# Layer B's q over all tokens as seven half-size block products, kept in DRAM, with z of the first token half ahead of it

## The chip, the core and the metric

The kernel runs on one core of a Trainium2 chip. The metric is device time in microseconds. Five engines matter here: TensorE (PE, its weight loads shown apart as PEld), VectorE (DVE), ScalarE (ACT), GpSimd (POOL) and SyncE (SP), which issues most DMAs. Each engine runs its own instructions in program order and waits on semaphores for the others.

## What is computed

1024 tokens of width 1024 in float32 pass one gated MLP layer (layer A), which also gives the shared k and v, and one sliding-window attention layer (layer B). The change touches layer B alone. Cut down, it is:

```python
h = h + rms_norm(gmlp_mixer(rms_norm(h, a_pre_g), ...), a_post_g)     # layer A
kv_in = rms_norm(h, kv_norm_g)
k, v = kv_in @ w_k, kv_in @ w_v                    # 4 heads of 64
q, z = jnp.split(rms_norm(h, b_pre_g) @ b_w_in, 2, axis=-1)
q = q * (HEAD_DIM ** -0.5)                         # 16 heads of 64
logits = q_block @ k_two_blocks.T + alibi          # blocks of 128, window 128
p = exp(logits - max(rowmax, sink)); denom = p.sum() + exp(sink - max)
o = (p @ v_two_blocks) / denom
h = h + rms_norm((o * jax.nn.silu(z)) @ w_out, b_post_g)
```

## The kernel before

**Arithmetic.** A float32 matrix product is made of three matmuls on operands split in two parts: hi, a copy rounded to the matmul's format (ACT, line 105 or 109), and lo, the rest (DVE, line 106 or 110). `mm3` issues hi by hi, hi by lo and lo by hi into one PSUM bank (lines 169 to 171). Layer A's three products are already seven half-size block products each for eight, with sums of blocks made on DVE and POOL by `add` (line 206). Layer B's are plain.

**Tokens.** The 1024 tokens are two halves of 512, h = 0 and 1. The normalised, transposed tokens of a half are `n`, a hi and lo tile of eight 128-row pieces by 512 tokens: `n0` comes from layer A's last stage, `n1` is made here. For n1 a token tile of 128 is scaled (`hb`, DVE, line 763), transposed by PE into PSUM (`nt`, line 769), and split into n_hi (ACT) and n_lo (DVE).

**Weights.** The class `Weights` holds a fixed list of 512 KB weight blocks in the order of use: q, kv, z for the first half, kv, q, z for the second, and at last the output weights. `wnext` hands out one block, splits the next into whi and wlo (lines 109 and 110, two of 128x512 each) and loads two further. Raw blocks live in a ring of three buffers, filled by SP's queue.

**Stages of layer B's front.** They are generators, so that a main stage can step a side stage between its groups of matmuls:

- `q_phase(0)`: 192 matmuls (`qz`, line 952 on). The side stage is `chain_a(1)`, the residual and norm of the second half's tokens (lines 746 to 758). Each of q's 128-row pieces leaves PSUM with a scale as hi (ACT, line 971) and lo (DVE, line 972) parts of 64 rows: q is kept as two tiles, each with hi in one half of its 128 rows and lo in the other.
- `kv_phase(0)`: k and v of the first half, with `norm_h1(1)` at its side.
- `z_phase(0)`: 192 matmuls; ACT takes z out of PSUM and applies SiLU (lines 981 and 984).
- `attn(0)`: eight units (two head groups by four blocks of 128 tokens). A unit is two score groups, each of eight matmuls (`s`, line 1050), DVE's masking and row maximum (lines 1055 and 1061) and ACT's exponentials (line 1065); a normalisation (lines 1070 and 1071); transposes (`pt`, line 1078) with POOL's selection (lines 1082 and 1083); values (`o`, lines 1097 and 1099); and the product with z and its split (lines 1103, 105 and 106). Stage i of the loop runs scores of unit i, transposes of unit i−1 and values of unit i−2. Between these, four calls of `more()` a stage step `fill`, which here is kv, q and half of z of the second half, 64 steps in all, spread evenly over 40 calls.
- `attn(1)` in the same way, with the rest of z and the output product of the first half as fill, and then the second half's output product to the end.

What sets the order: each engine's order is that of the generators' steps above, as the compiler's scheduler has arranged them; nothing at run time changes it. The names that recur below are `hb`, `n_hi`, `n_lo`, `q_slots` (a ring of result buffers), `qz`, `whi`, `wlo`, `raw_w`, `pr` (probabilities), `mx` and `dn` (row maximum and denominator), `kh`, `kl` and `vt` (k's parts and v).

Of the kernel before, what the change touches and what calls it, by code (L numbers as in the profile page):

```python
# [7 lines left out]
F32 = mybir.dt.float32  # L8
# [42 lines left out]
def tile_yoco(  # L51
# [60 lines left out]
    class Weights:  # L112


        def __init__(self):
            self.order = []
            q, z = ([(wqz[i, m:m + 4, :, kq * 256:kq * 256 + 256].rearrange("m p c -> p m c"), f"q{kq}")
                     for m in range(0, 8, 4) for kq in range(4)] for i in range(2))
# [3 lines left out]
            self.raw, self.done, self.at = [], [], 0  # L122

        def load(self, i):
            while len(self.raw) <= min(i, len(self.order) - 1):
# [4 lines left out]
        def split(self, i):  # L130
            while len(self.done) <= min(i, len(self.order) - 1):
# [627 lines left out]

    def norm_h1(h, n, yo, order=range(4)):  # L760
# [172 lines left out]
    bp = ctx.enter_context(tc.tile_pool(name="bp", bufs=1))  # L933
    bias = bp.tile([P, 4, P], F32, name="bias")
    nc.sync.dma_start(out=bias.rearrange("p a b -> p (a b)"), in_=consts[:, C_BIAS:C_BIAS + 512])
    mrg = bp.tile([P, P], F32, name="mrg")
    nc.sync.dma_start(out=mrg, in_=consts[:, C_MERGE:C_MERGE + P])
    neg = bp.tile([P, 1], F32, name="neg")
    nc.vector.memset(neg, -1e30)

    kh = [bp.tile([P, 2, S], F32R, name=f"kh{i}") for i in range(2)]

    kl = [bp.tile([P, 2, S], F32R, name="kl0")]
    qsc = bp.tile([P, 2], F32, name="qsc")
    nc.sync.dma_start(out=qsc, in_=consts[:, C_QS:C_QS + 2])
    snk = bp.tile([P, 4, 4], F32, name="snk")
    nc.sync.dma_start(out=snk.rearrange("p a b -> p (a b)"), in_=sinks.partition_broadcast(P))
    nc.vector.tensor_scalar(snk, snk, -1.0, None, ALU.mult)
    half = [slice(0, 64), slice(64, P)]
    vt = big.tile([P, NB, 256], F32, tag="P1_1", name="vt")  # L950

    def qz_four(h, which, m, n, evac):

        tag = "s" if (h, which, m) in ((0, 0, 4), (0, 1, 0)) else "mm"
        ps = [bank(tag, f"qz{h}_{which}_{m + i}") for i in range(4)]
# [10 lines left out]
    def q_phase(h, n, q):  # L966
        def evac(m, ps):
            for par in range(2):
                rw, ot = half[par], half[1 - par]
                g = qsc[rw, m // 4:m // 4 + 1]  # L970
                nc.scalar.activation(q[par][rw, m], ps[rw], AF.Copy, scale=g)
                nc.vector.scalar_tensor_tensor(q[par][ot, m], ps[rw], g, q[par][rw, m].bitcast(F32),  # L972
                                               ALU.mult, ALU.subtract)

        for m in range(0, 8, 4):
            yield from qz_four(h, 0, m, n, evac)

    def z_phase(h, n, z, m0, m1):
        def evac(m, ps):
            zt = z[m // 4]  # L980
            nc.scalar.activation(zt[:, m % 4], ps, AF.Copy)
            if m % 2 == 1:
                zs = zt[:, m % 4 - 1:m % 4 + 1]
                nc.scalar.activation(zs, zs, AF.Silu)

        for m in range(m0, m1, 4):
            yield from qz_four(h, 1, m, n, evac)

    def kv_phase(h, n):
        pk = [bank("mm", f"pk{h}_{i}") for i in range(2)]  # L990
        pv = [bank("mm", f"pv{h}_{i}") for i in range(2)]
# [114 lines left out]
    def attn(h, q, z, fill, total, late=0):  # L1106
        taken = [0, 0]
        n = 34 if late else 40
# [8 lines left out]
        for i in range(len(units) + 2):  # L1117
# [5 lines left out]
            more()  # L1123
            if 0 <= i - 1 < len(units):
# [79 lines left out]
    side = chain_a(1, yo, ss)  # L1204
    q0 = pair("P0", "q0")
    main = q_phase(0, n0, q0)
    step(main, main)
    for _ in main:
        step(side)
    drain(side)  # L1210
# [83 lines left out]
```

## Time and profile before

| what | us |
|---|---|
| median of 3 runs | 1050.68 |
| lowest and highest run | 1050.01, 1051.42 |
| the profiled execution | 1051.56 |
| its span in the trace | 1049.8 |

The mean granted TensorE clock of the profiled execution is 0.998. A trace row for one instruction gives its start, its length, engine, line, operation and tiles, and in brackets the idle time before it with what ended that. Matmuls overlap in PE's pipeline, so the distance from one start to the next, not the length, is what one costs. A row of groups ends with busy time and mean length in ns, then idle time before and its releaser. The stages in the trace: q of the first half from 654.1, kv from 697.6, z from 723.4, attention of the first half from 769 to 894.7, of the second half to 1005, then the rest of the output product to 1043 and the last stores.

### The profile page before, as it was taken

The numbers are of one execution on the slowest core, as the hardware profiler recorded it, in microseconds if no ns is written. First come the engines' busy times: TensorE is split into PE (matmuls) and PEld (weight loads), VectorE is DVE, ScalarE is ACT, GpSimd is POOL, SyncE is SP. The second block draws the span as 40 slices with busy tenths as digits, with TensorE's granted clock in tenths as the row PEclk, the third lists the DMA queues.
The fourth block names the chain that finished last, engine by engine and source line by source line (L and its number), as shares of the span: only waits on it lengthen the run. The fifth ranks groups of instructions, "written<-read, shape, count | busy, mean of one in ns | idle before, by whom it ended". The sixth has DMA issues, their size and how long they took to land.

```text
span 1049.8 us, 13661 instructions
## 1 busy us (share of the span) xinstructions
PE 1039.2 (99%) x4994; PEld 854.8 (81%) x4994; DVE 731.9 (70%) x1244; ACT 577.2 (55%) x989; POOL 195.2 (19%) x153
## 2 busy tenths in 40 slices
PE   9999999999999999999999999999999999999997
PEld 7888788888888888888888888888888777877776
DVE  6997466867768668677697587665247776667763
ACT  6683444555465565555444464654466665786631
POOL 0300003253342542530200000100001111011120
PEclk9999999999999999999999999999999999999999
DMA  8877252334333333347897642532222121211363
GB/s 310 271 282 269 101 177 88 116 105 143 124 121 116 132 124 117 108 137 272 322 352 270 201 160 93 200 102 86 95 81 71 51 81 61 81 61 61 121 220 120
DMA packets 80899, 157.56 MB, mean 150 GB/s; under 512 B 5824, under 2 KB 32704, under 8 KB 80832
## 3 DMA queue, kind: packets, MB, share of 16 engines
q1 hardware_dynamic: 76176, 147.75, 41.2%
q10 hardware_dynamic: 4656, 8.94, 2.4%
q8 instruction: 39, 0.64, 0.3%
q14 instruction: 28, 0.23, 0.1%
HBM read 125.21 MB, written 31.46 MB: 149 GB/s over the span
## 4 chain that ended last, share of the span: by engine, by line
PE 93%; DVE 4%; ACT 1%; issue 0%; DMA 0%; POOL 0%; DVEq 0%; POOLq 0%; ACTq 0%
PE ob L169 6%; PE ub L169 6%; PE ub L171 6%; PE ob L171 6%; PE ob L170 6%; PE ub L170 6%; PE qz L169 5%; PE qz L171 5%; PE qz L170 5%; PE uc L169 3%; PE uc L171 3%; PE uc L170 3%; PE s L1050 3%; PE sp L614 3%; PE vb L170 2%; PE vb L171 2%
## 5 line engine op out<-in xcount | busy, mean ns | idle before, releaser
L110 DVE SCALAR_TENSOR_TENSOR wlo<-raw_w,gn,whi 128x512 fp32r<-128x512 f32 x80 | 58.7, 758 | 62.2 <-ACT whi L109 62.0
L169 PE MATMUL qz<-n_hi,whi 128*128 128x512 f32 x256 | 101.0, 394 | 0.4 <-DVE q_lo L972 0.4
L171 PE MATMUL qz<-n_hi,wlo 128*128 128x512 f32 x256 | 100.0, 391 | 1.2 <-DVE wlo L110 1.2
L170 PE MATMUL qz<-n_lo,whi 128*128 128x512 f32 x256 | 99.8, 390 | 0.0
L109 ACT ACTIVATE whi<-raw_w,gn 128x512 fp32r<-128x512 f32 x80 | 54.9, 716 | 54.2 <-PE qz L170 35.0
L1065 ACT ACTIVATE pr<-pr,mx 128x129 f32<-128x129 f32 x128 | 50.0, 393 | 40.1 <-DVE mx L1061 40.0
L169 PEld LDWEIGHTS qz<-n_hi,whi 128*128 128x128 f32 x256 | 48.0, 188 | 16.6 <-issue 6.5
L105 ACT ACTIVATE uzhilo_g<-f 128x1024 fp32r<-128x1024 f32 x31 | 32.9, 1060 | 48.6 <-PE uc L171 42.7
L171 PEld LDWEIGHTS qz<-n_hi,wlo 128*128 128x128 f32 x256 | 48.0, 188 | 12.3 <-DVE wlo L110 2.1
L170 PEld LDWEIGHTS qz<-n_lo,whi 128*128 128x128 f32 x256 | 48.1, 188 | 9.3
L106 DVE TENSOR_TENSOR uzhilo_g<-f,uzhilo_g 128x1024 fp32r<-128x1024 f32 x31 | 39.0, 1257 | 19.9 <-ACT uzhilo_g L105 19.9
L209 ACT ACTIVATE uz_slots<-ub 128x512 f32<-128x512 f32 x48 | 28.3, 590 | 42.4 <-PE ub L171 39.0
L169 PE MATMUL ub<-T,whi_g 128*128 128x512 f32 x128 | 50.7, 396 | 0.0
L169 PE MATMUL ub<-T,uzhilo_g 128*128 128x512 f32 x128 | 50.5, 395 | 0.0
L171 PE MATMUL ub<-T,wlo_g 128*128 128x512 f32 x128 | 49.9, 390 | 0.0
L171 PE MATMUL ub<-T,uzhilo_g 128*128 128x512 f32 x128 | 49.9, 390 | 0.0
L170 PE MATMUL ub<-T,uzhilo_g 128*128 128x512 f32 x128 | 49.8, 389 | 0.0
L170 PE MATMUL ub<-T,whi_g 128*128 128x512 f32 x128 | 49.8, 389 | 0.0
L169 PE MATMUL uc<-T,uzhilo_g 128*128 128x512 f32 x124 | 48.9, 395 | 0.0
L170 PE MATMUL uc<-T,uzhilo_g 128*128 128x512 f32 x124 | 48.3, 389 | 0.0
L171 PE MATMUL uc<-T,uzhilo_g 128*128 128x512 f32 x124 | 48.3, 389 | 0.0
L105 ACT ACTIVATE whi_g<-raw_uz 128x1024 fp32r<-128x1024 f32 (+1 forms) x31 | 26.5, 854 | 36.7 <-PE ub L170 15.6
(332 smaller groups left out, 3071.4 us busy)
## 6 DMA issues: line engine op xcount, KB each, us to landing
raw_uz<-in_wuz_in_dram SPq DMA_DIRECT2D x32, 512.0 KB, 3.4
raw_w<-in_wqz_dram SPq DMA_DIRECT2D x32, 512.0 KB, 3.5
td<-uz_slots SPq DMA_DIRECT2D x56, 256.0 KB, 2.2
orawP2a<-td SPq DMA_DIRECT2D x28, 512.0 KB, 4.0
raw<-in_wv_in_dram SPq DMA_DIRECT2D x17, 512.0 KB, 4.8
vg<-vd SPq DMA_DIRECT2D x8, 1024.0 KB, 5.4
orawP2b<-in_wo_a_dram SPq DMA_DIRECT2D x16, 512.0 KB, 7.7
vraw<-in_wv_in_dram SPq DMA_DIRECT2D x13, 512.0 KB, 4.4
```

The costliest lines, as they stand in the source:

```text
L105: nc.scalar.activation(hi, src, AF.Copy)
L106: nc.vector.tensor_tensor(lo, src, hi.bitcast(F32), ALU.subtract)
L109: nc.scalar.activation(hi, src, AF.Copy, scale=g)
L110: nc.vector.scalar_tensor_tensor(lo, src, g, hi.bitcast(F32), ALU.mult, ALU.subtract)
L169: nc.tensor.matmul(out, lhsT=a_hi, rhs=b_hi, start=start, stop=False, skip_group_check=True)
L170: nc.tensor.matmul(out, lhsT=a_hi, rhs=b_lo, start=False, stop=False, skip_group_check=True)
L171: nc.tensor.matmul(out, lhsT=a_lo, rhs=b_hi, start=False, stop=stop, skip_group_check=True)
L209: nc.scalar.activation(out, a, AF.Copy)
L614: nc.tensor.matmul(psv[:, n], lhsT=d["vg"][:, 4 * j + n, i * P:(i + 1) * P], rhs=d["wc"], start=True, stop=True)
L1050: nc.tensor.matmul(pss[par][:, g, w0:256], lhsT=q[par][:, m, bs_], rhs=w[par][:, p, ks], start=g + k == 0, stop=g + k == 2, skip_group_che ...
L1065: nc.scalar.activation(pr[:, i], pr[:, i], AF.Exp, bias=mx[:, i:i + 1], scale=-1.0, accum_out=dn[:, i:i + 1])
```

## The change

q is computed for both halves at once. The 1024 by 1024 weight matrix and the tokens are taken as two by two blocks of 512, and Strassen's scheme (in Winograd's form) makes seven block products for eight. In pieces:

- `z_phase(0)` runs first, where q's first half ran. Its result goes to DRAM (`zd`, four stores) and comes back after the k/v stage.
- At its side run `chain_a(1)` and, new, `norm_sums`: the work of `norm_h1(1)` and the sums of token blocks that the products need (T5, T6, T4, T7; T1 to T3 are parts of n0 and n1). For each of four token tiles these are three subtractions and three lo splits on DVE, four additions and subtractions on POOL, and three hi splits on ACT, beyond n1's own.
- `q_tiles`: four quads of two 128-row weight blocks; each has seven products of 12 matmuls. DVE scales the raw weights by the norm's gain, POOL makes the weight sums, ACT and DVE split them. Results are summed from PSUM in six buffers and stored to DRAM (`qd`, 16 stores). The weights of its first quad are fetched and prepared at steps 22 and 27 of z.
- Buffers for this (`qp`) are closed after q, and the pool `bp` (masks, sink constants, kh, kl) is opened after that; it stood ahead of q before.
- `reload_q` brings a half of q back, four pieces of 512 KB, and makes the scaled hi and lo parts, two ACT and two DVE operations of 64x1024 a piece. The first half's pieces 0 and 1 are started in `kv_phase(0)` and one more piece in each stage of `attn(0)`: 2 and 3 of the first half, then the four of the second.
- `attn(0)` has 32 steps of fill for 64, kv and half of z; four of them run ahead of its first unit.

```diff
             kv = [(wkv[kp], f"kv{kp}") for kp in range(4)]
-            self.order += q + kv + z + kv + q + z
+            self.order += z + kv + kv + z
...
+    def norm_sums(n, yo, first):
...
+        for t in (2, 3, 0, 1):
+            ts_ = slice(t * P, (t + 1) * P)
+            xt = st.tile([P, D], F32, tag="xt", name=f"hb1_{t}")
+            nc.vector.tensor_scalar(xt, yo[t], r1[1][:, t:t + 1], None, ALU.mult)
+            yield
...
+            for kq in range(2):
...
+                split(n[0][:, ks, ts_], n[1][:, ks, ts_], ps)
+                if kq == 0:
+                    add(t1, ps, n_0[0][0][:, :, ts_].bitcast(F32), ALU.subtract)
+                    add(t1, t1, n_0[1][0][:, :, ts_].bitcast(F32), ALU.subtract, nc.gpsimd)
+                else:
+                    add(t3[:, :, ts_], ps, n[0][:, 0:HT, ts_].bitcast(F32), ALU.subtract)
+                    add(t2, ps, t1, ALU.subtract)
+                    add(t4, n_0[0][1][:, :, ts_].bitcast(F32), t2, ALU.subtract, nc.gpsimd)
+                    add(t3[:, :, ts_], t3[:, :, ts_], n[1][:, 0:HT, ts_].bitcast(F32), ALU.subtract, nc.gpsimd)
+                    add(t4, t4, n_0[1][1][:, :, ts_].bitcast(F32), ALU.add, nc.gpsimd)
+                yield
+            for m, src in ((6, t2), (5, t1)):
+                split(T[m][0][:, :, ts_], T[m][1][:, :, ts_], src)
+            yield
+            split(T[4][0][:, :, ts_], T[4][1][:, :, ts_], t4)
+            yield
...
+        for i in range(2):
+            split(*(a[:, 2 * i:2 * i + 2] for a in T[7]), t3[:, 2 * i:2 * i + 2])
+        yield
...
-    def q_phase(h, n, q):
...
+    def q_tiles():
...
+        def scaled(r):
+            rv = r.rearrange("p (k c) -> p k c", k=KT)
+            add(rv, rv, gn[:, G_BPRE:G_BPRE + KT].unsqueeze(2).broadcast_to([P, KT, P]), ALU.mult)
...
+        def prep1(q):
+            if q < 4:
+                r0, r1 = raws[q]
+                ops[q] = {}
+                scaled(r0)
+                pieces_of(q, r0, "q1", 1, 2)
+                scaled(r1)
+
+        def prep2(q):
...
+                add(s1, a21, a22, ALU.add, nc.gpsimd)
+                add(s2, s1, a11, ALU.subtract, nc.gpsimd)
+                pieces_of(q, f, "q2", 6, 5)
+                add(s3, a11, a21, ALU.subtract, nc.gpsimd)
+                add(s4, a12, s2, ALU.subtract, nc.gpsimd)
...
+        for q in range(5):
...
+                product(q, 1, b, True)
...
+                product(q, 2, a, True)
+                add(c00, c00, a, ALU.add)
+                store(q, 0, 0, c00)
+                prep1(q + 1)
...
+            product(q, 6, b, False)
...
+            product(q, 5, cc, True)
+            prep2(q + 1)
+            fetch(q + 2)
+            product(q, 7, b, False)
...
+    def reload_q(h, q):
+
+        for i in range(4):
+            r = raw_tile(f"q{h}_{i}").rearrange("p (m t) -> p m t", m=2)
+            nc.sync.dma_start(out=r, in_=qd[h][i])
+            ms = slice(2 * i, 2 * i + 2)
             for par in range(2):
                 rw, ot = half[par], half[1 - par]
...
+                nc.scalar.activation(q[par][rw, ms], r[rw], AF.Copy, scale=g)
+                nc.vector.scalar_tensor_tensor(q[par][ot, ms], r[rw], g, q[par][rw, ms].bitcast(F32),
                                                ALU.mult, ALU.subtract)
...
-    def attn(h, q, z, fill, total, late=0):
+    def attn(h, q, z, fill, total, late=0, first=0, side=iter(())):
         taken = [0, 0]
+        for _ in range(first):
+            step(fill)
...
+            step(side)
             if 0 <= i - 1 < len(units):
                 units[i - 1].transposes()
...
-    main = q_phase(0, n0, q0)
+    side = chain(chain_a(1, yo, ss), norm_sums(n1, yo, n0))
...
+    main = z_phase(0, n0, z0, 0, 8, keep=True)
+    qs = q_tiles()
     step(main, main)
-    for _ in main:
+    for i, _ in enumerate(main):
         step(side)
+        if i in (22, 27):
+            step(qs)
     drain(side)
...
+    drain(qs)
+    qp_ctx.close()
...
-    fill = chain(kv_phase(1, n1), q_phase(1, n1, q1), z_phase(1, n1, z1, 0, 4))
-    attn(0, q0, z0, fill, 64)
+    fill = chain(kv_phase(1, n1), z_phase(1, n1, z1, 0, 4))
+    attn(0, q0, z0, fill, 32, first=4, side=chain(side, reload_q(1, q1)))
```

Two places show how the instructions stand on DVE. The first is where the second half's first token tile is scaled, beside q's matmuls before and beside z's now. In the rows `hb_2` is token tile 2 scaled, `r_1_90` the norm's factor, `wlo` the lo part of a weight block and `qz_0_0` q's first bank. Before:

```order
L178 TENSOR_SCALAR r_1_90<-s_1_4999 128x4
L763 TENSOR_SCALAR hb_2_5318<-yoa_3_4273,r_1_90 128x1024
L110 SCALAR_TENSOR_TENSOR wlo_5097<-raw_w_5024,gn,whi_5096 128x4x128 x2
L972 SCALAR_TENSOR_TENSOR q_hi<-qz_0_0_4959,qsc,q_hi 64x512
L763 TENSOR_SCALAR hb_3_5352<-yoa_3_4273,r_1_90 128x1024
L972 SCALAR_TENSOR_TENSOR q_hi<-qz_0_1_4960,qsc,q_hi 64x512
```

Now, further on in the same stage, with `qT_5055`, `qT_5056` and `qT_1_5058` the lo parts of T5, T6 and T4, and `t_3` the temporaries t1 and t2 of token tile 3:

```order
L208 TENSOR_TENSOR q_slots<-nt_3_1_5166,n_hi 128x4x128
L208 TENSOR_TENSOR t_3_5149<-nt_3_1_5166,t_3_5148 128x512
L106 TENSOR_TENSOR qT_5055<-t_3_5148,qT_5055 128x4x128
L110 SCALAR_TENSOR_TENSOR wlo_5196<-raw_w_5067,gn,whi_5195 128x4x128
L106 TENSOR_TENSOR qT_5056<-t_3_5149,qT_5056 128x4x128
L110 SCALAR_TENSOR_TENSOR wlo_5196<-raw_w_5067,gn,whi_5195 128x4x128
L106 TENSOR_TENSOR qT_1_5058<-q_slots,qT_0_5057 128x4x128
L779 TENSOR_SCALAR hb_0_5217<-yoa_2_4272,r_1_90 128x1024
L110 SCALAR_TENSOR_TENSOR wlo_5255<-raw_w_5128,gn,whi_5254 128x4x128 x2
L779 TENSOR_SCALAR hb_1_5284<-yoa_2_4272,r_1_90 128x1024
L106 TENSOR_TENSOR n_lo<-nt_0_0_5227,n_hi 128x4x128
L208 TENSOR_TENSOR t_0_5225<-nt_0_0_5227,n_hi 128x512
```

The evacuations of q (line 972) have left this stage; the sums, n's lo parts and T's lo parts have come in, and hb of tiles 0 and 1 stands behind T4's lo part of tile 3, whose source `q_slots` POOL writes.

The second place is DVE in the first half's attention. `pr`, `mx` and `s` are a unit's probabilities, maxima and scores, `z_0` the gate. Before:

```order
L1061 ISA pr_1_6365,mx_1_6366<-s_1_01_6370,bias,snk 128x128
L1061 ISA mx_1_6366 128x1
L1103 TENSOR_TENSOR z_0_5296<-o_0_6389,z_0_5296 128x4x128
L106 TENSOR_TENSOR q_lo<-z_0_5296,q_hi 128x4x128
L110 SCALAR_TENSOR_TENSOR wlo_6410<-raw_w_6281,gn,whi_6409 128x4x128 x2
L972 SCALAR_TENSOR_TENSOR q_hi<-qz_0_0_6207,qsc,q_hi 64x512
L1038 COPY pr_1_6495<-snk 128x8
L972 SCALAR_TENSOR_TENSOR q_lo<-qz_0_0_6207,qsc,q_lo 64x512
```

Now, in the third unit's stage:

```order
L1223 RECIPROCAL dn_0_6285<-dn_0_6285 128x8
L1214 ISA pr_0_6381,mx_0_6382<-s_0_00_6385,bias,snk 128x128
L1214 ISA mx_0_6382 128x1
L1224 TENSOR_TENSOR pr_0_6283<-pr_0_6283,dn_0_6285 128x8x128
L1214 ISA pr_0_6381,mx_0_6382<-s_0_00_6385,bias,snk 128x128
L1214 ISA mx_0_6382 128x1
L1125 SCALAR_TENSOR_TENSOR q_hi<-raw_q_3_6321,qsc,q_hi 64x1024
L1125 SCALAR_TENSOR_TENSOR q_lo<-raw_q_3_6321,qsc,q_lo 64x1024
L1214 ISA pr_0_6381,mx_0_6382<-s_0_01_6386,bias,snk 128x128
```

In place of the evacuations from PSUM, 16 of 64x512 for the second half, stand the splits of pieces that come back from DRAM (line 1125 of the changed kernel), 12 of 64x1024 in this attention, among the units' own operations.

More of the change, by code (lines that the diff above doesn't have):

```diff
@@ L973, in evac, with z_phase @@
                                                ALU.mult, ALU.subtract)
[L975 to L978 removed]
+            yield
+    def z_phase(h, n, z, m0, m1, keep=False):
         def evac(m, ps):
```

179 lines of the change are left out of this document (140 added, 39 removed).

## The prediction

> **What bounds the kernel now.** I read the page's busy times and its chain first, then busy time by stage, because a share of the whole says little about one stage.
>
> ```profile
> span 1049.8 us, 13661 instructions
> PE 1039.2 (99%) x4994; PEld 854.8 (81%) x4994; DVE 731.9 (70%) x1244; ACT 577.2 (55%) x989; POOL 195.2 (19%) x153
> PE 93%; DVE 4%; ACT 1%; issue 0%; DMA 0%; POOL 0%; DVEq 0%; POOLq 0%; ACTq 0%
> ```
>
> PE is busy in 99% of the span, and the chain that ended last runs over PE for 93% of it. So a matmul that goes shortens the time, as long as the other engines still keep ahead of PE. The windows show how near they are (window, its length, then busy time of PE, PEld, DVE, ACT and POOL, the granted clock, DMA).
>
> ```profile
> 26.20:52.50 26.30, 26.30 (x117) 21.43 (x116) 25.67 (x28) 15.79 (x21) 10.20 (x3) 1.00 0.81 271
> 654.00:697.60 43.60, 42.35 (x186) 34.44 (x185) 26.92 (x38) 22.36 (x38) 3.82 (x3) 1.00 0.48 162
> 723.40:769.00 45.60, 45.60 (x209) 37.97 (x208) 15.48 (x22) 22.30 (x35) 0.00 (x0) 1.00 0.32 104
> 769.00:894.70 125.70, 125.25 (x681) 99.70 (x680) 90.63 (x254) 81.38 (x215) 15.29 (x14) 1.00 0.21 68
> 1043.00:1046.00 3.00, 0.07 (x1) 0.00 (x0) 1.99 (x4) 0.69 (x2) 0.54 (x1) 1.00 0.00 1
> 1046.00:1049.80 3.80, 0.00 (x0) 0.00 (x0) 0.24 (x1) 0.00 (x0) 0.00 (x0) 0.58 0.38 140
> ```
>
> Layer B's first q stage (654 to 697.6) and z stage (723.4 to 769) leave DVE and ACT much room. In the first half's attention (769 to 894.7) DVE has work for 90.6 of 125.7 us: PE's matmuls of kv, q and z hide it. The change takes out the q part of that cover.
>
> **Part 1: matmuls removed, −10.9 us.** q over 1024 tokens is 2 × 192 matmuls before, and 4 × 7 × 12 = 336 after: 48 fewer of the same shape.
>
> ```profile
> 654.10 0.39 PE L169 MATMUL qz<-n_hi,whi 128*128 128x512 f32 x1
> 661.80 0.39 PE L170 MATMUL qz<-n_lo,whi 128*128 128x512 f32 x1
> ```
>
> PE's timeline has 34 starts from the first of these rows to the second: 7.70/34 = 0.2265 us each, and 48 × 0.2265 = 10.9 us. Other PE work is only moved: 32 transposes go from the kv stage into the z stage.
>
> **Part 2: the sums before q can start, +10 us (5 to 17).** q's products now need sums of both token halves. So the second half's normalisation (hb), its transposes, and the operands T4 to T7 must be done within the z stage, where there was slack. On DVE, between hb of tile 2 and the lo part of the first q weight (wlo_q_0, which the fifth matmul of q needs), stand 4 hb, 8 half weight splits (L110), 32 subtractions of 128x512 and 4 operations of 128x1024. Their prices are steps from one start to the next:
>
> ```profile
> 672.11 0.17 DVE L178 TENSOR_SCALAR r<-s 128x4 f32<-128x4 f32 x1 [1.28 <-ACT junk_h L183]
> 673.40 0.76 DVE L763 TENSOR_SCALAR hb<-yoa,r 128x1024 f32<-128x1024 f32 x1 [1.12 <-POOL r L179]
> 674.07 1.41 DVE L110 SCALAR_TENSOR_TENSOR wlo<-raw_w,gn,whi 128x512 fp32r<-128x512 f32 x2
> 704.71 1.29 DVE L106 TENSOR_TENSOR n_lo<-nt,n_hi 128x512 fp32r<-128x512 f32 x2
> 857.39 0.20 DVE L1070 RECIPROCAL dn<-dn 128x8 f32<-128x8 f32 x1 [0.90 <-ACT pr L1065]
> 857.63 1.23 DVE L1071 TENSOR_TENSOR pr<-pr,dn 128x1024 f32<-128x1024 f32 x1
> 858.78 1.41 DVE L110 SCALAR_TENSOR_TENSOR wlo<-raw_w,gn,whi 128x512 fp32r<-128x512 f32 x2
> ```
>
> hb takes 0.67 (673.40 to 674.07); a pair that lasts 1.41 with 0.75 for its second gives 0.66 for an L110; a pair of 1.29 gives some 0.61 for a 128x512 subtraction; 857.63 to 858.78 gives 1.15 for 128x1024. The sum is 2.7 + 5.3 + 19.5 + 4.6 = 32.0 us. It can't begin before hb of tile 2, at 673.4 in the trace, since the norm ahead of it is as it was: DVE is done at 705.4 at the earliest. PE comes to that matmul at 654.1 + 192 × 0.2265 + 4 × 0.87 (transposes) + 4 × 0.2265 = 702.0. So at least 3.4 us are lost even with DVE packed.
>
> It isn't packed: four POOL operations a tile stand between its DVE operations.
>
> ```profile
> L206 POOL TENSOR_TENSOR f<-raw_uz,raw_uz 128x512 f32<-128x512 f32 x15 | 19.2, 1281 | 127.2 <-DVE uzhilo_g L106 127.2
> L206 POOL TENSOR_TENSOR uz_slots<-uz_slots 128x512 f32<-128x512 f32 x17 | 27.7, 1631 | 0.5
> 301.25 2.16 POOL L206 TENSOR_TENSOR uz_slots<-uz_slots 128x512 f32<-128x512 f32 x1
> L105 ACT ACTIVATE q_hi<-z 128x512 fp32r<-128x512 f32 x8 | 5.0, 623 | 5.7 <-DVE z L1103 5.7
> L105 ACT ACTIVATE uzhilo_g<-f 128x1024 fp32r<-128x1024 f32 x31 | 32.9, 1060 | 48.6 <-PE uc L171 42.7
> ```
>
> Sixteen at 1.28 to 1.63 are 20.5 to 26.1 us. The first follows the first t1 on DVE at some 677.4. In DVE's order T4's lo of tile 3 stands ahead of hb of tile 0, so POOL idles behind its eighth operation until ACT's hi of T4 (0.62) and DVE's lo, hb, two L110, hb, n_lo and t1 (0.61 + 0.67 + 1.32 + 0.67 + 0.61 + 0.61) have passed: 5.1 us. POOL is then done at 703 to 709, and T4's lo, T7's two pieces and wlo_q_0 follow (0.61 + 3 × 1.15 = 4.1, and 0.6 of ACT): 708 to 713. I take 710.5, 8.5 us behind PE. A second, smaller wait is at q's matmul 31, on the first weight sums: from wlo_q_0 on, a scaled weight (1.15), three POOL operations (3.8 to 4.9), ACT's hi (1.06) and DVE's lo (1.15) take 7.2 to 8.3 us, against 26 matmuls, 5.9: 1.5 more. **The middle is +10**; the low end is 3.4 + 1.3, about 5 (POOL's part wholly hidden in the z stage), the high end has 16 × 0.4 us more, towards the 2.16 row, +17.
>
> The Trainium skill (SBUF — State Buffer, section "Who interferes with whom") says that a DVE instruction with two SBUF inputs contends with a GpSimd instruction that reads SBUF. The lo parts of T4 to T7 are such instructions. The rows 1281, 1631 and 2.16 for one operation are in keeping with that, though they don't show its cause; by the rule the sum would lie at the upper end of this part, without it near the lower.
>
> Once q runs, its DVE work (12 adds, 15 weight pieces, 7 scalings: 7.3 + 17.3 + 8.1 = 32.7 us) and POOL's 16 sums (20.5 to 26.1) lie beside 336 × 0.2265 = 76.1 us of matmuls: no further loss.
>
> **Part 3: attention without q's matmuls, +10 us (5 to 20).** Before, 64 steps of matmuls are spread over this attention; now 32, of which four run ahead of it, at the same rate per call. Six unit stages hold the last of them and five or six pieces of q reloaded from DRAM, each two ACT and two DVE operations of 64x1024.
>
> ```profile
> 716.97 0.40 PE L169 MATMUL pk<-n_hi,whi 128*128 128x512 f32 x1
> 719.79 0.40 PE L169 MATMUL pk<-n_hi,whi 128*128 128x512 f32 x1
> ...
> 702.41 0.87 PE nt L769 x8
> ...
> 846.74 0.94 PE s L1050 x8
> ...
> 859.91 1.01 PE o L1097 x4
> 860.93 0.86 PE o L1099 x4
> ...
> 659.71 2.48 DVE L753 SCALAR_TENSOR_TENSOR yoa<-yoa,rpa,xa 128x1024 f32<-128x1024 f32 x2 [1.19 <-POOL rpa L179]
> 838.06 0.76 DVE L1055 COPY_PREDICATED s<-mrg,s 128x256 f32<-128x256 uint32 x2
> 839.81 0.68 DVE L1103 TENSOR_TENSOR z<-o,z 128x512 f32<-128x512 f32 x1
> L1019 DVE TENSOR_TENSOR kl<-pk,kh 64x512 fp32r<-64x512 f32 x4 | 2.8, 688 | 0.5 <-ACT kh L1018 0.4
> ```
>
> PE in these six stages: 6 kv pairs of 2.82 (716.97 to 719.79), 16.9; 48 z matmuls, 10.9; 13 score groups of 0.94, 12.2; 5 transpose groups of 0.87, 4.4; values 6.6 (mostly 1.01 + 0.86); 51.0 us. DVE: 12.5 score groups of 1.75 (838.06 to 839.81), 21.9; 6 normalisations of 1.39 (857.39 to 858.78), 8.3; 8 gating operations and splits of 0.61, 4.9; 9 weight splits of 0.66, 5.9; 6 copies and subtractions for k and v of 0.61, 3.7; 12 reloads, for which the trace has only the 128x1024 form (2.48 for two, 1.2 from start to start), 14.4; 59.1 us. **DVE takes PE's place as the bound here.** Less two score groups (3.5 us) by which DVE may start ahead or end behind, 59.1 − 51.0 − 3.5, about 5 us, are lost with DVE packed. It wasn't packed before:
>
> ```profile
> DVE dn L1070 <- ACT pr L1065: 6.0, 7, 0.9
> ```
>
> Seven waits of the normalisation for the exponentials (0.9 us each at most) stood there at no cost to PE; six of them now count, 5 us: +10. The high end doubles the excess, where ACT and DVE wait for each other. The stage as a whole is near balance too: DVE 90.6, less 16 evacuations of q (0.74 each, 11.8) and 16 weight splits of q (11.3), plus 14.4, is 82; PE 125.7 less 43.5 (192 matmuls), less 5.6 (two kv pairs, now ahead), plus 7 for z matmuls that had run after, is 83.6.
>
> **Part 4: edges and DRAM, +0.5 us (0 to 3).** 16 stores of q, four of z, eight reloads of q and four of z stand on SP's queue, eight weight loads leave it.
>
> ```profile
> td<-uz_slots SPq DMA_DIRECT2D x56, 256.0 KB, 2.2
> raw_w<-in_wqz_dram SPq DMA_DIRECT2D x32, 512.0 KB, 3.5
> ```
>
> A store and its reload take 2.2 + 3.5 us, and the first half's kv (8 × 2.82 = 22.6 us) lies between the last store and the first scores. Behind a waiting reload stand the weight loads, two stages ahead of their use. The pool for masks and k/v begins where q's ends, so its constants load later, also in that cover; uncovered, one trip costs 5.7, of which I keep 3 as the high end.
>
> **Sum.** −10.9 + 10 + 10 + 0.5 = +9.6. The profiled execution took 1051.56 (its span and 1.8 around it), so 1061.2; the runs' median, 1050.68, is 0.88 lower: **1060.3 us**.
>
> **Rivals.** (a) *The cover holds* (faster): in 26.2 to 52.5 DVE was busy 25.67 of 26.30 us and PE lost nothing, so DVE can be packed. Then only 5 us (part 2's floor) and 2 us (waits at units' edges) are lost: −10.9 + 7 = −4, 1046.7. It decides if the two losses together stay under 10.9. Against it: that window has few instructions without waits between engines, here each tile goes DVE, PE, ACT, DVE, POOL, DVE. (b) *Only the z stage loses*: DVE's lead carries attention, −10.9 + 10 + 4 = +3, 1053.8. (c) *The clock falls too*: the last rows of the windows show a granted clock of 1.00 in the first 3 us without matmuls and 0.58 in the next 3.8. A wait of over 3 us before q would then slow the matmuls behind it: 0.42 × 3.8 = 1.6 us a gap, two or three gaps, and high ends of parts 2 and 3: 1066 to 1076. For it speaks the length of part 2's wait; against it that waits for single tiles may split it. The Trainium skill (TensorE: Matmul & The Clock Gate, section "What's actually happening") has the clock at half speed after an idle window of about 3.4 us; the two rows agree with it. (d) *The change doesn't do what it says*: no fewer matmuls issued, or a DRAM trip in the path each unit (8 × 2.2 = 18 us): above 1068.
>
> **How the numbers follow.** About 0.2% (2 us) is what a measurement of this kernel can tell from no change. Forecast (1055 to 1066) 0.47; (a) 0.20, of it 0.17 below 1048.5; between (a) and (b), 1048.5 to 1053, 0.08; (b) 0.12; (c) 0.10; (d) 0.03. Faster 0.20 with the edges of (a), same 0.08, slower 0.72. The sum's own ends are 1050 and 1080; the range 1046 to 1075 reaches down to (a) and leaves the far ends out.
>
> **What would show it.** Part 1: some 4946 matmuls, 0.2265 us apart. Part 2: a PE gap of 5 to 12 us where z ends, released by DVE (wlo_q_0 or T's lo), and POOL's sums back to back ahead of it. Part 3: between kv of the first half and the end of the z matmuls PE under 90% busy and DVE over 85%, with PE's scores and transposes released by DVE. If PE is full in that stretch, part 3 is wrong; if z's end has no gap, part 2 is wrong and the time falls below 1050. (c): granted clock under 0.95 behind the gap.

## The result, and the profile after

The changed kernel takes **1076.55 us** (median of 4 runs, 1074.9 to 1077.34) against 1050.78 (4 runs) of the kernel before on the same chip: a ratio of 1.0239, 95% interval 1.0227 to 1.0251, or 25.8 us slower. The forecast was slower by 9.6 us, 1060.3 us in a range of 1046 to 1075. The page of the changed kernel, first its span, the busy times and the granted clock, then the chain:

```profile
span 1075.6 us, 13692 instructions
PE 1041.8 (97%) x4946; PEld 850.4 (79%) x4946; DVE 768.6 (71%) x1258; ACT 587.1 (55%) x989; POOL 248.8 (23%) x185
...
PEclk9999999999999999999999999889999989999999
...
PE 83%; DVE 7%; ACT 4%; issue 3%; POOL 2%; DMA 1%; POOLq 0%; SPq 0%; DVEq 0%; ACTq 0%
```

The 48 matmuls are gone (4994 records before, 4946 now). PE fell from 99% to 97% of a longer span and from 93% to 83% of the chain: other engines now end PE's waits. Which waits, the table of PE's waits says (line, releaser: us in total, how many, the longest), from 640 to 935 us, which holds layer B's front and the first half's attention. First all that the kernel before has there, then the seven largest of the changed kernel:

```profile
PE qz L171 <- DVE wlo L110: 1.2, 2, 0.7
PE qz L169 <- DVE q_lo L972: 0.4, 1, 0.4
```

```profile
PE qb L171 <- ACT whi_q L105: 5.4, 1, 5.4
PE o L1250 <- POOL pc L1236: 4.7, 3, 2.3
PE z L173 <- DVE wlo L110: 4.6, 3, 3.3
PE pt L1231 <- DVE pr L1224: 3.7, 2, 2.0
PE s L1203 <- ACT pc L1232: 2.1, 2, 2.0
PE qc L171 <- ACT qhilo_q L105: 1.8, 1, 1.8
PE nt L787 <- DVE hb L779: 1.6, 1, 1.6
```

Four of them (`nt`, `z`, `qb`, `qc`) stand between the start of z and q's first quad, 13.4 us; three (`pt`, `s`, `o`) in the attention, 10.5 us. The stages by windows of the changed kernel (length, then busy time of PE, PEld, DVE, ACT and POOL, granted clock, DMA): z up to q's first matmul, q and the first half's k/v, the first half's attention, and the first 64.5 us of it apart.

```profile
654.00:717.50 63.50, 51.71 (x227) 40.91 (x225) 52.35 (x64) 33.29 (x58) 25.92 (x18) 0.92 0.35 127
717.50:827.50 110.00, 108.20 (x516) 90.89 (x517) 52.67 (x62) 43.30 (x59) 27.87 (x18) 0.97 0.42 142
827.50:927.80 100.30, 89.39 (x485) 66.11 (x483) 85.11 (x234) 77.71 (x199) 17.00 (x14) 0.95 0.24 79
827.50:892.00 64.50, 55.25 (x310) 41.85 (x309) 55.36 (x155) 47.62 (x127) 8.66 (x7) 0.92 0.25 83
```

DVE is busy for 52 of 63 us in the first of them, where before it had had 27 of 44. To compare kernels I count a stretch's **loss**: its length, less its matmuls at the prediction's prices (0.2265 us for 512 columns, some 0.118 for 256, 0.87 for eight transposes). Some matmul records may be missing, so a loss is good to about 1 us.

| stretch | before | after |
|---|---|---|
| first stage of layer B up to the next | 1.9 | 16.2 |
| from there to the first scores | 0.2 | 6.0 |
| first half's attention | 3.3 | 19.7 |
| the rest | 2.3 | 2.2 |

The first stage before ends where k/v's first matmul stands in PE's timeline, at 699.5, not at the 697.6 that the list of stages and the prediction's window give; k/v's end is 725.4 for 723.4 likewise.

The losses grew by 14.3 + 5.8 + 16.4 − 0.1 = 36.4 us; less 10.9 for the matmuls that is 25.5, the measured difference.

### The profile page after: what moved, and what is told of

The parts are those of the page before. It is cut to its first block, busy times and chain, and to the rows that moved or that the text cites. A ratio compares the mean times of both kernels' runs of the same rounds, so it can differ in the third digit from the quotient of the medians.

```text
span 1075.6 us, 13692 instructions
## 1 busy us (share of the span) xinstructions
PE 1041.8 (97%) x4946; PEld 850.4 (79%) x4946; DVE 768.6 (71%) x1258; ACT 587.1 (55%) x989; POOL 248.8 (23%) x185
## 4 chain that ended last, share of the span: by engine, by line
PE 83%; DVE 7%; ACT 4%; issue 3%; POOL 2%; DMA 1%; POOLq 0%; SPq 0%; DVEq 0%; ACTq 0%
PE ob L171 6%; PE ub L171 5%; PE ub L173 5%; PE ob L172 5%; PE ob L173 5%; PE ub L172 5%; PE uc L173 3%; PE uc L172 3%; PE uc L171 3%; PE sp L616 3%; PE vb L172 2%; PE vb L173 2%; PE vb L171 2%; PE oc L171 2%; PE oc L172 2%
## 5 line engine op out<-in xcount | busy, mean ns | idle before, releaser
L173 PE MATMUL z<-n_hi,wlo 128*128 128x512 f32 x128 | 51.7, 404 | 4.6 <-DVE wlo L110 4.6
L171 PE MATMUL z<-n_hi,whi 128*128 128x512 f32 x128 | 52.7, 412 | 0.2 <-ACT z L1132 0.2
L172 PE MATMUL z<-n_lo,whi 128*128 128x512 f32 x128 | 51.3, 401 | 0.0
L208 POOL TENSOR_TENSOR f<-raw_uz 128x512 f32<-128x512 f32 x15 | 20.1, 1340 | 127.5 <-DMA raw_uz<-in_wuz_in_dram 85.4
L208 POOL TENSOR_TENSOR f<-raw_uz,raw_uz 128x512 f32<-128x512 f32 x15 | 19.2, 1281 | 128.5 <-DVE uzhilo_g L106 128.5
L110 DVE SCALAR_TENSOR_TENSOR wlo<-raw_w,gn,whi 128x512 fp32r<-128x512 f32 x48 | 38.6, 832 | 11.2 <-ACT whi L109 10.9
L1235 POOL TENSOR_SCALAR_AFFINE_SELECT pp<-pc 128x1024 f32<-128x1024 f32 x14 | 16.0, 1141 | 129.9 <-ACT pc L1232 129.9
L109 ACT ACTIVATE whi<-raw_w,gn 128x512 fp32r<-128x512 f32 x48 | 32.8, 715 | 23.1 <-PE oc L173 7.6
```

The lines of the kernel that those rows point to most:

```text
L109: nc.scalar.activation(hi, src, AF.Copy, scale=g)
L110: nc.vector.scalar_tensor_tensor(lo, src, g, hi.bitcast(F32), ALU.mult, ALU.subtract)
L171: nc.tensor.matmul(out, lhsT=a_hi, rhs=b_hi, start=start, stop=False, skip_group_check=True)
L172: nc.tensor.matmul(out, lhsT=a_hi, rhs=b_lo, start=False, stop=False, skip_group_check=True)
L173: nc.tensor.matmul(out, lhsT=a_lo, rhs=b_hi, start=False, stop=stop, skip_group_check=True)
L208: (eng or nc.vector).tensor_tensor(out, a, b, op)
```

## The experiments

Each kernel was timed beside the kernel before on the same chip; a time is compared by its ratio.

**1. POOL's additions made on DVE.** The changed kernel has four additions a token tile on POOL for the sums. The edit, at all four:

```diff
-                    add(t1, t1, n_0[1][0][:, :, ts_].bitcast(F32), ALU.subtract, nc.gpsimd)
+                    add(t1, t1, n_0[1][0][:, :, ts_].bitcast(F32), ALU.subtract)
...
```

> The 16 additions for T4 to T7 that POOL makes in the z stage are made on DVE instead. Theory (POOL's part is the cause: it stretches DVE's operations with two SBUF operands from 0.68 to 1.2 to 2.4 us and makes hand-overs): such DVE operations go back to about 0.7 us, the 16 cost 16 x 0.6 = 9.6 us, DVE has 32 + 9.6 us from 672.9 and ends wlo_q_0 at about 715 instead of 718.7; q starts 3 to 4 us earlier, the whole is 1069 to 1074. Rival (the amount of DVE work alone sets the end): 9.6 us more, 1083 to 1088.

Measured: 1078.46 us, ratio 1.0246 (1.023 to 1.0263), the same as the changed kernel. Neither theory's time came. The groups of DVE's work from 672 to 719 us show why. The changed kernel:

```profile
L106 DVE TENSOR_TENSOR qT<-t,qT 128x512 fp32r<-128x512 f32 x8 | 11.1, 1393 | 1.0 <-ACT qT L105 1.0
L110 DVE SCALAR_TENSOR_TENSOR wlo<-raw_w,gn,whi 128x512 fp32r<-128x512 f32 x8 | 7.7, 996 | 0.0
L106 DVE TENSOR_TENSOR n_lo<-nt,n_hi 128x512 fp32r<-128x512 f32 x8 | 5.4, 680 | 1.2 <-ACT n_hi L105 1.2
...
L208 DVE TENSOR_TENSOR raw_q<-raw_q,gn 128x1024 f32<-128x1024 f32 x2 | 3.5, 1770 | 0.0
```

With the additions on DVE:

```profile
L106 DVE TENSOR_TENSOR qT<-t,qT 128x512 fp32r<-128x512 f32 x8 | 5.5, 688 | 3.4 <-ACT qT L105 3.4
L110 DVE SCALAR_TENSOR_TENSOR wlo<-raw_w,gn,whi 128x512 fp32r<-128x512 f32 x8 | 5.7, 746 | 0.0
L208 DVE TENSOR_TENSOR raw_q<-raw_q,gn 128x1024 f32<-128x1024 f32 x3 | 3.5, 1220 | 0.0
```

The stretching is real: the same lo part takes 1393 ns with POOL at work and 688 without. Over these groups it comes to 5.6 + 2.0 + 1.1 = 8.7 us, and the 16 additions cost DVE about the same, 16 × 0.6. So POOL's help was worth nothing here: what it took off DVE it gave back by slowing it, and q's first matmul stands at 718.4 for 717.5.

**2. PE kept busy in front of q.**

```diff
+    fillers = bank("s", "fillers")
+    for _ in range(24):
+        nc.tensor.matmul(fillers[:, 0:P], lhsT=ones, rhs=ones, start=True, stop=True)
     drain(qs)
```

> 24 matmuls of 128x128 whose result nobody reads, put on PE between z and q, where PE waits 5.4 us. Theory (the wait lowers the granted clock, and that alone makes the first nine matmuls of q start 0.43 apart): with PE kept busy they start 0.23 apart; q's second wait then grows by some of the 1.9 us won, so the whole gains 0 to 3 us, 1073 to 1077. Rival (something else slows these matmuls, such as DVE, POOL and ACT writing beside them): they stay 0.43 apart, and the time is 1076 to 1078.

Measured: 1079.7 us, ratio 1.0265 (1.025 to 1.0281), over both ranges. The clock theory is right on its mechanism. PE's timeline in the changed kernel at q's first matmuls (start, length):

```profile
717.51 0.80 PE L171 MATMUL qb<-n_hi,whi_q 128*128 128x512 f32 x1 [5.38 <-ACT whi_q L105]
718.11 0.63 PE L172 MATMUL qb<-n_lo,whi_q 128*128 128x512 f32 x1
718.54 0.63 PE L171 MATMUL qa<-n_hi,whi_q 128*128 128x512 f32 x1
```

and with the fillers, there and at q's second wait (the 24 fillers leave 48 records):

```profile
710.77 5.52 PE L1383 MATMUL fillers<-ones 128*128 128x128 f32 x48
...
718.16 0.40 PE L172 MATMUL qb<-n_lo,whi_q 128*128 128x512 f32 x1
718.40 0.40 PE L173 MATMUL qb<-n_hi,wlo_q 128*128 128x512 f32 x1
...
727.38 0.50 PE L171 MATMUL qb<-qT,qhilo_q 128*128 128x512 f32 x1 [4.48 <-ACT q_slots L211]
```

Starts are 0.43 us apart without, 0.24 with them, and the granted clock from 714 to 721 us is 1.00 for the changed kernel's 0.53. But the second wait grew from 1.79 to 4.48: PE came there earlier, but ACT's copy of q's first bank, behind its work on the weight sums, stands at 726.8 as without the fillers (726.6). Of the time that the half clock took here, nothing could be won. Why the median is some 2.7 us over the changed kernel's stays open; the profiled execution, 1077.99, is the fastest of the four.

**3. The second half's reload later.** In the attention's loop:

```diff
-            step(side)
+            if i < 2 or i > 4:
+                step(side)
```

> The second half's four reload pieces (8 DVE operations of 1.31 us and 8 of ACT of 1.15 us from start to start) are moved from unit stages 2 to 5 of the first half's attention to its stages 5 to 8. Theory (they stand in DVE's and ACT's queues ahead of the normalisations and of k's and v's copies out of PSUM, for which PE waits): the loss in this attention falls from 17 us to 5 to 10, and the whole is 1064 to 1070. Rival (q's matmuls were the cover for the units' own chain of engines, and without them PE waits anyway): 1074 to 1078. Between them, if the waits only move to stages 5 to 8: 1070 to 1074.

Measured: 1075.18 us (1072.68 to 1078.27), ratio 1.0233 (1.0216 to 1.025): no change that the measurement tells, in the rival's range. The waits moved, as the middle case has it, but to no gain: `z` for ACT's copy 2.0 and `o` for DVE 2.8 us in place of some of the `pt` and `o` waits. Stages 5 to 8 had no more room for these operations than stages 2 to 5.

**4. q split ahead of its stores.** `store` writes hi and lo, `reload_q` is four DMAs a piece:

```diff
+            split_scaled(hi, lo, c, qsc[:, q // 2:q // 2 + 1])
-            nc.sync.dma_start(out=qd[j][q][:, i], in_=c)
+            nc.sync.dma_start(out=qd[j][0][q][:, i], in_=hi.bitcast(F32))
+            nc.sync.dma_start(out=qd[j][1][q][:, i], in_=lo.bitcast(F32))
...
-                nc.scalar.activation(q[par][rw, ms], r[rw], AF.Copy, scale=g)
-                nc.vector.scalar_tensor_tensor(q[par][ot, ms], r[rw], g, q[par][rw, ms].bitcast(F32),
-                                               ALU.mult, ALU.subtract)
+                nc.sync.dma_start(out=q[par][rw, ms].bitcast(F32), in_=qd[h][0][i][rw])
+                nc.sync.dma_start(out=q[par][ot, ms].bitcast(F32), in_=qd[h][1][i][rw])
```

> q's scaling and its split in hi and lo are made before the stores, in the q stage (16 operations each of ACT and DVE of 128x512), both parts are kept in DRAM, and the reload is DMA alone: 12 DVE and 12 ACT operations leave the first half's attention, 4 of each leave the k/v stage. Theory (these operations are what PE waits behind): the loss in attention falls from 17 to 2 to 6 us, q's stage loses 0 to 2 more, and the whole is 1060 to 1066. Rival (cover): the waits for normalisation, copies and POOL stay, 1073 to 1078.

Measured: 1064.4 us, ratio 1.0122 (1.0107 to 1.0137), by the ratios 12.3 us under the changed kernel, as the theory had it. In this kernel the first half's attention runs from 828.8 to 912.5:

```profile
828.80:912.50 83.70, 80.06 (x472) 61.84 (x470) 67.90 (x220) 60.93 (x183) 16.61 (x14) 1.00 0.50 121
```

PE is busy for 80.1 of 83.7 us (96%) where it was for 89.4 of 100.3 (89%), and the clock no longer falls here. The loss in the attention is 6.3 for 19.7 us; the z stage keeps its 16.2. The same splits, done in the q stage, cost 1 us there. They are not the same operations: 32 of 128x512 stand for 32 of 64x1024, and take 13.0 us of DVE and 11.5 of ACT for 20.8 and 18.4. So this experiment changes their place and their length together.

**5. POOL's additions left out.** The four `add` lines of POOL are deleted, and T4 is split from t2.

> POOL's 16 additions for T3 to T7 are left out altogether (so q is not the reference's), all else as in the changed kernel. Theory (POOL beside DVE and the hand-overs between them make the part of the sum that was too small): DVE's operations on two SBUF operands fall from 1.2 to 2.4 us to 0.7, nothing waits for POOL, DVE has the 32 us of the sum from 672.9 and ends wlo_q_0 at 705 to 707; q starts at 706 to 709 for 717.5, the whole is 1062 to 1068. Rival (DVE's and ACT's own queues hold q back even so): q starts behind 713, the whole is 1071 to 1077.

Measured: 1066.34 us, ratio 1.0138 (1.0121 to 1.0155), 10.6 us under the changed kernel, in the theory's range. q starts at 708.0 for 717.5, and the two losses ahead of the scores fall from 16.2 and 6.0 to 6.2 and 4.8; the attention keeps 21.3.

**6. k/v of the first half ahead of q,** on top of experiment 4.

```diff
-            self.limit = 8
+            self.limit = 12
...
+    for i, _ in enumerate(kv_phase(0, n0)):
+        if i % 3 < 2:
+            step(side)
+        if i in (4, 9):
+            step(qs)
     drain(side)
...
-    attn(0, q0, z0, fill, 32, first=4, side=chain(side, reload_q(1, q1)))
+    attn(0, q0, z0, fill, 26, first=8, side=chain(side, reload_q(1, q1)))
```

k and v go through DRAM, since the pool for k's parts opens only after q's buffers are closed.

> On top of the early split, the first half's k/v matmuls (26.6 us of PE) stand between z and q, so that the sums have 73 us of matmuls beside them for 47; their results go to DRAM and come back after q, and eight steps of the second half's k/v run ahead of the attention for four. Theory (the sums lacked cover, and nothing else holds q back): z, k/v and q lose 2 to 5 us together for 22, the attention loses 4 to 8, the way back of k and v 0 to 4, and the whole is 1044 to 1052, at or under the kernel before. Rival (the hand-overs make PE wait wherever the sums stand): z, k/v and q lose 10 or more, the whole is 1054 to 1062.

Measured: 1067.23 us, ratio 1.015 (1.0135 to 1.0166). The sums are better covered: z, k/v and q lose 14.5 us for 22 to 23 by the same count. But the attention loses 18.0 for 6.3. Its first wait, on PE's timeline:

```profile
829.67 0.41 PE L1214 MATMUL s<-kl,q_lo 128*128 128x256 f32 x1
833.07 1.30 PE L1242 MATMUL pt<-ident,pr 128*128 128x128 f32 x5 [2.98 <-DVE pr L1235]
```

Three score groups run back to back, and PE has nothing else until the first unit is normalised.

**7. The same, paced otherwise:** `first=6` of 32, the side steps spread over z, and k/v in the other four banks.

> As the kernel with k/v ahead of q, with three things set otherwise: its k/v banks are those that the transposes used (so that they don't wait for z's evacuation), the sums are spread over z by their own pace, and six steps of the second half's k/v run ahead of the attention, of 32 spread as in the changed kernel. Theory (early cover in the attention counts, and the bank wait was avoidable): z, k/v and q lose 6 to 8 us for 10, the attention 7 to 10 for 15, the whole is 1055 to 1061. Rival (the way of k, v and q back from DRAM sets the start of the attention): what is won there is waited for ahead of the first scores, 1063 to 1068.

Measured: 1067.74 us, ratio 1.0157 (1.0142 to 1.0172): the rival's range. The attention's loss fell by some 3 us, that ahead of it rose by 2.8. The rival's reason is not what the trace shows: PE waits 1.2 us for q's way back, where it had waited 0.5, but 3.5 for ACT's parts of the k/v weights ahead of q.

**8. Less to fill with.** Experiment 4 with one line changed:

```diff
-    attn(0, q0, z0, fill, 32, first=4, side=chain(side, reload_q(1, q1)))
+    attn(0, q0, z0, fill, 26, first=8, side=chain(side, reload_q(1, q1)))
```

> The early split kernel with eight steps of the second half's k/v ahead of the attention for four, and 26 for 32 in the spread: 5.6 us of matmuls stand ahead of the units and no longer between them, nothing else. Theory (cover counts too, beside the reload's operations): the loss in the attention rises from 3.7 to 8 to 14 us, the whole is 1068 to 1075. Rival (with the reload's operations gone the units' chain has room): 1063 to 1066.

Measured: 1067.71 us, ratio 1.0158 (1.0141 to 1.0175), 3.8 us over experiment 4, between the two ranges. Cover counts, but the attention's loss rose by 2.3 only, less than I expected; with each ratio good to some 1.7 us, the 3.8 is good to about 2.4. The fill is that of experiment 6, so the other 9.4 of the 18.0 us lost there belong to what else differs: k and v come back from DRAM, and no k/v stage stands between q's last store and the scores. No run separates these.

**9. Experiment 7 with the additions on DVE.**

> As the paced kernel with k/v ahead of q, and the 16 additions on DVE. Theory (with enough matmuls beside them the sums are best on one engine, without POOL's stretching of DVE): z, k/v and q lose 3 to 6 us, the whole is 2 to 4 us under the paced kernel. Rival (DVE's 9.6 us more are felt): 2 to 6 us over it.

Measured: 1062.72 us, ratio 1.0116 (1.0101 to 1.0131), 4.3 us under experiment 7 (the theory said 2 to 4). The loss ahead of the attention fell by 5.7 us. With k/v's matmuls beside the sums, all of them on DVE were better than DVE and POOL at once; in experiment 1, without that cover, they were no better.

**10 and 11. Half of the reload's work left out.** In 10 the `scalar_tensor_tensor` of `reload_q` is replaced by a DMA into the same place, in 11 the `activation`.

> The reload's lo parts are not computed: DMA fills their places with q's raw values (so the scores are not the reference's). DVE loses its 16 operations of 1.31 us, ACT keeps its 16 of 1.15 us. Theory (DVE's queue is what PE waits behind in the attention): nearly as much is won as by the early split, the attention loses 4 to 8 us for 17, the whole is 1063 to 1068. Rival (ACT's queue, in which the exponentials and the copies of k and of the transposes stand behind the reload's hi parts): 1071 to 1077.

> The reload's hi parts are not computed: DMA fills their places with q's raw values (so the scores are not the reference's). ACT loses its 16 operations, DVE keeps its 16. Theory (DVE's queue): 1071 to 1077. Rival (ACT's queue): 1063 to 1068. If both count, since each lo waits for its hi and each exponential for its maximum, both kernels come to 1067 to 1072.

Measured: 1072.29 us for 10, ratio 1.0197 (1.0174 to 1.0221), just over the middle case and at the lower end of the rival's; 1082.28 us for 11, ratio 1.0301 (1.0284 to 1.0318), outside all three. In 11 the lo parts make up for the raw hi parts, so the scores are the reference's after all. Neither kernel is a clean test, since its DMA put a new wait at the head of a queue. The waits from 800 us on, of ACT in experiment 10, then of DVE and ACT in experiment 11:

```profile
ACT q_hi L1124 <- DMA raw_q<-qd: 3.9, 1, 3.9
```

```profile
DVE q_hi L1125 <- DMA raw_q<-qd: 8.0, 3, 4.1
...
ACT pr L1218 <- DVE mx L1214: 25.2, 15, 7.0
```

In 11 DVE stood for 8.0 us at lo parts whose piece had not landed, with the maxima of the next scores behind them in its queue, and ACT's exponentials waited 25.2 us for those. How the 12.3 us of experiment 4 divide between ACT and DVE stays open.

**12. PE kept busy in the attention.** Eight fillers each, in the bank that the next matmuls write, ahead of two units' `pt` and two units' `o`.

> Eight matmuls of 128x128 (1.8 us) that nobody reads are put ahead of two units' transposes and two units' values in the first half's attention, where PE waits 1.4 to 2.3 us at a time and the granted clock falls. Theory (the fall of the clock costs time there, since scores, transposes and values at half speed stand in the chain that everything waits for): matmuls behind these waits run at full speed, the whole is 2 to 5 us faster, 1072 to 1075. Rival (what is lost to the clock would be waited for anyway): 1076 to 1079.

Measured: 1076.66 us, ratio 1.0244 (1.0229 to 1.026): the rival. The windows from 855 to 865 and to 875 us, first of the changed kernel, then of this one:

```profile
855.00:865.00 10.00, 7.84 (x41) 5.76 (x37) 9.00 (x20) 9.89 (x25) 0.00 (x0) 0.83 0.31 105
865.00:875.00 10.00, 5.73 (x14) 2.87 (x16) 9.58 (x22) 5.97 (x15) 2.85 (x2) 0.66 0.16 52
```

```profile
855.00:865.00 10.00, 9.09 (x67) 7.26 (x65) 9.01 (x23) 9.70 (x25) 0.00 (x0) 1.00 0.31 105
865.00:875.00 10.00, 7.86 (x38) 6.04 (x38) 9.80 (x21) 6.24 (x15) 2.33 (x2) 0.83 0.16 54
```

The clock rises from 0.83 and 0.66 to 1.00 and 0.83, and the kernel takes the same time; DVE and ACT are busy in turn for 90 to 98% of these windows. It is not a clean test. From 835 to 845 us the clock now falls to 0.83, where it was 1.00, and over the whole attention it is 0.97 for 0.95: the fall was moved more than removed.

**13. Experiments 4 and 5 in one.**

> POOL's 16 additions left out (so q is not the reference's) and q split ahead of its stores, in one kernel. If the two causes are separate they add up: 10.6 us and 12.2 us less than the changed kernel's 1076.6, so 1052 to 1056, and what is left is 1 to 5 us over the kernel before in spite of 10.9 us of matmuls fewer. If both measure the same loss (waiting that only moves from one stage to the other), the second brings little: 1060 to 1064.

Measured: 1052.23 us (median of 10), ratio 1.0009 (1.0 to 1.0019). The two causes are separate and add up within the intervals: 10.6 + 12.3 = 22.9, measured 24.2 us under the changed kernel. The same three stages of this kernel, at their own times:

```profile
655.10:706.00 50.90, 47.57 (x225) 39.00 (x224) 43.57 (x66) 34.53 (x61) 2.01 (x2) 1.00 0.45 161
706.00:815.90 109.90, 107.78 (x516) 89.65 (x517) 60.52 (x72) 47.05 (x68) 30.69 (x18) 0.98 0.61 192
815.90:899.60 83.70, 80.08 (x471) 61.86 (x469) 67.90 (x220) 60.92 (x183) 16.62 (x14) 1.00 0.50 121
```

Even with the additions for nothing and the reload as mere DMA, the losses (3.9, 5.9 and 6.3 us in the three stretches, 10.7 more than before) eat the 10.9 us of matmuls. No kernel of this study that computes q in seven products beats the one before; the best of those that leave nothing out is experiment 9.

## Why the prediction was right in its direction and wrong in its size

The measured 1076.55 us lies above the range. The middles of parts 2 and 3 were too small by 10.1 and 6.4 us, and part 2 alone passed its own high end.

**Part 1, the matmuls (−10.9): right.** 48 records fewer, at the same spacing wherever PE doesn't wait.

**Part 2, the sums before q (+10; 5 to 17): this is the term that failed.** The two stretches lost 20.1 us more than before. The order was as argued: the last lo parts of T7 and wlo_q_0 stand behind POOL's last addition and set when q can begin. These rows of the changed kernel, POOL's, DVE's and ACT's timelines, show POOL's longest idle time and the end of the chain:

```profile
697.82 1.30 POOL L208 TENSOR_TENSOR t<-t,n_lo 128x512 f32<-128x512 f32 x1 [7.15 <-DVE t L208]
...
711.81 2.13 POOL L208 TENSOR_TENSOR q_slots<-q_slots,n_lo 128x512 f32<-128x512 f32 x1
...
714.63 2.96 DVE L106 TENSOR_TENSOR qT<-q_slots,qT 128x512 fp32r<-128x512 f32 x3
717.51 1.22 DVE L106 TENSOR_TENSOR wlo_q<-raw_q,whi_q 128x1024 fp32r<-128x1024 f32 x1
...
713.97 1.58 ACT L105 ACTIVATE qT<-q_slots 128x512 fp32r<-128x512 f32 x2 [2.33 <-POOL q_slots L208]
715.45 1.07 ACT L1132 ACTIVATE z<-z 128x512 f32<-128x512 f32 x2
716.40 1.06 ACT L105 ACTIVATE whi_q<-raw_q 128x1024 fp32r<-128x1024 f32 x1
```

POOL ended at 713.9 where I had 703 to 709, wlo_q_0 at 718.7 where I had taken 710.5. The step that failed is "The sum is 2.7 + 5.3 + 19.5 + 4.6 = 32.0 us": I priced DVE's operations by rows in which POOL stood still, and let the overlap stretch POOL's alone ("16 × 0.4 us more, towards the 2.16 row"). By the groups of experiment 1 it also stretched DVE's, by 8.7 us. POOL's sixteen operations took 24.1 us, within my 20.5 to 26.1; but POOL stood idle among them four times, 12.8 us in all, each time for DVE, where I had one idle time of 5.1. Experiment 5 shows what the 32.0 us were worth without POOL: there the two stretches lose 11.0 us, 8.9 more than before, for "3.4 + 1.3" at my low end (three scaled weights stand ahead of wlo_q_0 there, the sum has one). The rule of the Trainium skill that I weighed there (SBUF — State Buffer, section "Who interferes with whom") speaks of both engines; I used it on one. The trace agrees with it: 1393 ns against 688 for a lo part with two SBUF operands, while n_lo, which reads PSUM, stayed at 680.

Nor is the loss one gap where z ends, as I had it. PE was 10.8 us behind before its wait of 5.4 us began (at 712.1, for 701.3 by the prices): it had waited 4.6 us for the lo parts of z's own weights, which stood on DVE among the stretched sums, and 1.6 for hb, and part of the rest is the low clock from 690 to 697 us.

One more thing was not in the sum: ACT's queue. q's first matmul needs whi_q, and that stood on ACT behind T4's and T7's hi parts, which waited 2.33 us for POOL, and behind z's evacuation. So PE's wait names ACT, not DVE as I had said.

**Part 3, the attention (+10; 5 to 20): right in kind, too small.** 16.4 us more were lost, inside the bounds. I had 59.1 us of DVE's work beside 51.0 of PE's in six unit stages; the window of 64.5 us, about that stretch, has DVE busy for 55.4 and PE for 55.3, both 86%, in the ranges that I named for it. What I had too small was what stands behind the reload's operations. On DVE's and PE's timelines of the changed kernel (PEld is a weight load):

```profile
856.00 1.28 DVE L1125 SCALAR_TENSOR_TENSOR q_hi<-raw_q,qsc,q_hi 64x1024 fp32r<-64x1024 f32 x1
857.31 1.28 DVE L1125 SCALAR_TENSOR_TENSOR q_lo<-raw_q,qsc,q_lo 64x1024 fp32r<-64x1024 f32 x1
...
859.10 1.22 DVE L1224 TENSOR_TENSOR pr<-pr,dn 128x1024 f32<-128x1024 f32 x1
...
860.47 1.51 PE L1231 MATMUL pt<-ident,pr 128*128 128x128 f32 x8 [1.96 <-DVE pr L1224]
...
871.83 0.29 PEld L171 LDWEIGHTS z<-n_hi,whi 128*128 128x128 f32 x1 [1.61 <-DVE kl L1172]
```

A unit's normalisation comes 2.6 us later for the two lo parts ahead of it, and PE waits 1.96 for it. The copies of k and v out of PSUM stand in the same queues, so z's matmuls, which need their banks, come only at 871.8, released by DVE's lo part of k. I had named DVE as the releaser of scores and transposes; it is that of the transposes, while scores wait for ACT's copy `pc` (2.1 us) and the values, the largest of these waits, for POOL's selection (4.7). Experiment 4 gives the price of the reload's operations in their old place and form: the attention's loss falls by 13.4 of the 16.4 us, q's stage pays 1 of it back, and the kernel is 12.3 us faster. Of what is left, experiment 8 shows only that less cover costs some: 5.6 us of matmuls taken from between the units made 3.8 us.

**Part 4 (+0.5): right.** In the changed kernel PE waits for nothing from 765 us to its first scores, k/v stage included, and the round trips of q and z show in no wait of PE.

**The rivals.** (a) and (b) were wrong: both stages lost. (d) was wrong too: the 48 matmuls went, and none of PE's waits up to the end of the first half's attention is for a DMA. (c) came nearest, its 1066 to 1076 ends just under the measured time, but by parts 2 and 3 more than by the clock, as far as the runs show. The granted clock did fall:

```profile
690.00:697.00 7.00, 5.98 (x20) 4.58 (x19) 5.75 (x8) 2.84 (x5) 0.68 (x1) 0.53 0.40 141
714.00:721.00 7.00, 3.49 (x8) 2.81 (x9) 6.85 (x7) 6.44 (x9) 1.00 (x1) 0.53 0.19 76
868.00:875.00 7.00, 5.07 (x10) 2.34 (x12) 6.67 (x16) 3.06 (x10) 1.81 (x2) 0.51 0.24 75
```

Matmuls at half speed make up some of the loss. Experiment 2 took away the fall ahead of q, and the next wait grew and the time did not fall: there the low clock only filled time in which PE would have waited. Experiment 12 moved part of the fall in the attention, and the time stayed; that points the same way without settling it. The fall inside z no run took away by itself. There, from 691.94 to 696.23 us, six matmuls and eight transposes took 4.3 us, 2.2 by the prices, and behind these transposes ends POOL's longest idle time. By these rows up to some 2 us of part 2's loss may be the clock's own, an estimate that is not tested.

## What to carry to other kernels

Price an operation by a row in which the other engine works as it will after the change: two elementwise operations with SBUF operands, on DVE and POOL at once, cost here as much as both on DVE. When matmuls are taken away, count what they had covered on the other engines' queues, and put the work that a result still needs (a scale, a split) where matmuls remain, ahead of a trip through DRAM rather than behind it and, as experiment 4 did, on all 128 partitions. To tell whether a low clock costs time, keep PE busy in the wait and see whether the end moves, and whether the clock now falls elsewhere.

## What the runs showed of the hardware that was not expected

A DVE operation with two SBUF operands of 128x512 took 688 ns alone and 1.1 to 1.8 us beside POOL's, 1393 in the mean; one with an operand in PSUM stayed at 680. The clock fell without a long idle stretch: in the attention it was 0.57 from 861 to 865 us, behind a single wait of 1.96 us, where the prediction had reckoned with waits of over 3 us only.
